# Larger pieces in the halved feed-forward of a two-layer trunk, and modulation vectors spread otherwise over its two stages

## The chip, the cores and the metric

One core of a Trainium2 chip. The metric is the time of one execution in microseconds (us), lower is better; "before" is the median of three runs.

## The reference, cut to what matters

Two layers work on a latent stream x (512 tokens) and a context stream y (256 tokens), both of width 1024. Each layer does a half-step, a mixer and a second half-step. Nine vectors per layer (shift, scale, gate for each of the three) come from `silu(c) @ w_mod[l]` for the latents and `silu(c_ctx) @ w_mod[l]` for the context.

```python
mx = split(silu(c) @ w_mod[l] + b_mod[l], 9)        # my: the same from c_ctx
x = x + 0.5 * mx[2] * swiglu(modulate(rmsnorm(x), mx[0], mx[1]), w1, w3, w2)   # y with my
hx = modulate(rmsnorm(x), mx[3], mx[4])             # hy with my
x = x + mx[5] * mixer(hx, hy);   if not last: y = y + my[5] * ...
x = x + 0.5 * mx[8] * swiglu(modulate(rmsnorm(x), mx[6], mx[7]), ...)
if not last: y = y + 0.5 * my[8] * ...
```

In the last layer the context takes part in the first half-step and in the mixer's keys and values only; `my[5]` to `my[8]` of that layer are not used.

## The kernel before, in words

Activations lie with the features on the partitions. Every fp32 product is made of three fp32r matmuls (`mm3`, L164 to L166) from a high and a low part of each operand; ACT casts the high part of a weight block (L159), DVE subtracts for the low part (L160), up to LOOKAHEAD = 3 blocks ahead. d_ff = 2816 is cut into 22 tiles of 128.

Four feed-forwards run in turn: `ffn` for layer 0's first, `ffn_halved` for layer 0's second and layer 1's first (these two are called stage one and stage two below), `ffn` for layer 1's second. In `ffn_halved` the first WHOLE = 4 tiles are computed plainly; meanwhile DVE and ACT make 24 tiles of differences (T). The other 18 are computed by `up_halved`, which replaces eight block products by seven, each over 384 of the 768 tokens, with DVE and ACT combining results in between (L774, L788, L789, L795 to L803). After every SUB = 2 tiles (the last piece has 4), `down` multiplies g by w2 into PSUM tiles of eight banks, in groups of four (two output tiles, two streams): first with the first tile of the piece for all four, then with the second. Every PSUM result is evicted by ACT with its gate (`add_kept`, L229, tile xpart) and added by POOL's accumulating DMA (L231) to x, which is parked in DRAM (xkept). The last piece adds to x in SBUF on DVE instead.

One pool of 45 slots of 128x512 holds T, g, xpart, the intermediate halves, the vectors' accumulators and x. A halved tile's g takes two slots for the latents and, with its neighbour, two for the context.

The modulation vectors are made beside this on DVE. `mod_chunks` is a generator that loads w_mod in 512 KB chunks through SP's queue into two buffers (wm) and, at a pace in the kernel's own clock of PE work, adds each chunk to two accumulators, one per stream (L319, L321: four instructions per chunk). Four chunks make a half vector, which `mod_fold` transposes and reduces (L329, L330); two halves go through one small matmul (`mod_sums`). The load of chunk i+1 is issued behind the adds of chunk i-1, one buffer being freed by them. Engines work in program order, so an instruction that waits holds up all behind it on its engine.

Stage one carries five vectors of layer 1 at pace 7.4, stage two the other four at pace 9.0. That clock counts 42.8 us for two halved tiles with their down part.

Of the kernel before, what the change touches and what calls it, by code (L numbers as in the profile page):

```python
# [20 lines left out]
DEPTH = 2  # L21
DFF = 2816
NF = DFF // P
PIECES = (4, 4, 4, 4, 2, 4)
# [5 lines left out]
CTX, LAT = 0, 1  # L30
# [10 lines left out]
HK, HN, SUB, WHOLE = KD // 2, NT // 2, 2, 4  # L41
# [3 lines left out]
def per_block(n):  # L45

    return 2 if n * P * 2 <= 1024 else 1
# [34 lines left out]
class Kernel:  # L82
# [229 lines left out]
        yield  # L312
        self.mod_sums(l, j, (half,), rows[:, :32])

    def mod_add(self, acc, raw, k):
        for v in range(2):
            s = self.sc[:, k, v : v + 1]
            if k == 0:
                self.nc.vector.tensor_scalar(acc[v], raw, s, None, op0=ALU.mult)  # L319
            else:  # L320
                self.nc.vector.scalar_tensor_tensor(acc[v], raw, s, acc[v], op0=ALU.mult, op1=ALU.add)  # L321

    def mod_fold(self, acc, rows):

        nc = self.nc
        rv = rows.rearrange("p (v b) -> p v b", v=2)
        for v in range(2):
            t = self.slot("mturn")
            nc.vector.transpose(t, acc[v])  # L329
            nc.vector.tensor_reduce(rv[:, v], t.rearrange("p (b i) -> p b i", i=32), axis=mybir.AxisListType.X, op=ALU.add)  # L330
# [33 lines left out]
    def mod_chunks(self, ljs, pace):  # L364

        nc = self.nc
        steps = [(l, j, half, kk) for l, j in ljs for half in range(2) for kk in range(4)]

        def load():
            raw = self.wide("wm").rearrange("p (k n) -> p k n", k=2)  # L370
            nc.sync.dma_start(raw, self.ins["w_mod"][steps.pop(0)])
            return raw

        after = load()
        for l, j in ljs:
            rows = self.tiny(64, "mrow")
            for half in range(2):
                acc = [self.slot("macc") for _ in range(2)]
                for kk in range(4):
                    raw, after = after, load() if steps else None  # L380
                    yield -pace
                    for k in range(2):
                        self.mod_add(acc, raw[:, k], kk * 2 + k)
                self.mod_fold(acc, rows[:, half * 32 : half * 32 + 32])
            yield 11.71
            self.mod_sums(l, j, (0, 1), rows)

# [138 lines left out]
    def weight_order(self):  # L526

        ins = self.ins

        def halved(l, s):  # L530
            f0 = 0
            for npc in PIECES:
                w2 = ins["w2"][l, s, :, f0 * D : (f0 + npc) * D].rearrange("p (d f n) -> p d f n", d=KD, f=npc)
                sub = npc if f0 + npc == NF else SUB
                for a in range(0, npc, sub):
                    for f in range(f0 + a, f0 + a + sub):
                        both = [ins["w13"][l, s, f, :, m * 1024 : (m + 1) * 1024] for m in range(2)]
                        if f < WHOLE:
                            yield from both
                        else:  # L540
                            yield both
                    per = 8 // sub
                    for d in range(0, KD, per):
                        yield w2[:, d : d + per, a : a + sub]
                f0 += npc

        def ffn(l, s):
            f0 = 0
            for npc in PIECES:
                for f in range(f0, f0 + npc):  # L550
                    for m in range(2):
                        yield ins["w13"][l, s, f, :, m * 1024 : (m + 1) * 1024]
                n = npc * P * per_block(npc)
                for c in range(f0 * D, (f0 + npc) * D, n):
                    yield ins["w2"][l, s, :, c : c + n]
                f0 += npc

        for l in range(DEPTH):
            yield from (halved if (l, 0) in HALVED else ffn)(l, 0)
            for i in range(4, 8) if l < DEPTH - 1 else range(4):  # L560
                yield ins["w_feat"][l, i]
            for i in range(4) if l < DEPTH - 1 else range(4, 8):
                yield ins["w_feat"][l, i]
            for i in range(4):
                yield ins["w_tok"][l, i]
            for i in (10, 11, 12, 13, 8, 9, 14, 15, 16, 17):
                yield ins["w_feat"][l, i]
            for i in range(2):
                for dt2 in range(KD // 2):
                    yield ins["w_out"][l, i, dt2]  # L570
            yield from (halved if (l, 1) in HALVED else ffn)(l, 1)
# [236 lines left out]
    def ffn_halved(self, l, s, h, starts, grps, ends, done):  # L808
        nc = self.nc
        idx = 2 * s  # L810
        accs = {}
        T = {i: [[None] * HK for _ in range(2)] for i in (2, 3, 4)}
        f0 = 0
        while f0 < NF:
            g = self.empty()
            n = SUB if f0 < NF - PIECES[-1] else PIECES[-1]
            last = f0 + n == NF
            per = 8 // n

            def load():  # L820
                for st in (CTX, LAT):
                    self.load_x(st, self.kept[st])

            if f0 < WHOLE:
                if f0 == 0:
                    ws = {f: self.w13() for f in range(n)}
                    for grp in starts[:-1]:
                        self.up(ws, range(n), h, g, grp)
                    self.need(starts[-1])
                    task = self.spawn(self.differences(h, T), 1.0)  # L830
                for f in range(n):
                    if f0:
                        ws = {f: self.w13()}
                    for grp in grps if f0 else starts[-1:]:
                        self.up(ws, [f], h, g, grp)
                if f0 + n == WHOLE:
                    self.drain(task)
                    self.first_difference(h)
            else:
                for f in range(n):  # L840
                    self.up_halved(f, h, T, g, load if last and f == n - 1 else None)
            w2 = []

            def down(dt, grp, ps, fs):
                self.products([(ps, w2[dt // per], dt % per * n * P + fs[0] * P)], g, grp, fs, fs[0] == 0, fs[-1] == n - 1)

            if last:
                w2 = [self.weights() for _ in range(KD // per)]
                for grp in ends:
                    for dt in range(KD):  # L850
                        ps = self.psum("down")[:, : grp[2]]
                        down(dt, grp, ps, range(n))
                        xd = self.xs(dt, grp)
                        nc.vector.scalar_tensor_tensor(xd, ps, self.gate(l, idx, grp[0], dt), xd, op0=ALU.mult, op1=ALU.add)
                        self.square(dt, grp, accs)
                    done(grp, accs)
            else:
                for d in range(0, KD, 2):
                    if d % per == 0:
                        w2.append(self.weights())  # L860
                    these = [(dt, grp, self.psum("down")[:, : grp[2]]) for grp in grps for dt in (d, d + 1)]
                    for fs in ((0,), (1,)):
                        for dt, grp, ps in these:
                            down(dt, grp, ps, fs)
                    for dt, grp, ps in these:
                        self.add_kept(dt, grp, ps, self.gate(l, idx, grp[0], dt))
            f0 += n
# [447 lines left out]
    def run(self):  # L1315
        nc = self.nc
# [62 lines left out]
        later = self.spawn(self.mod_chunks([(0, j) for j in range(3, 9)], 6.0), 80.0)  # L1379
        for l in range(DEPTH):  # L1380
# [9 lines left out]
            if not last:  # L1390
                self.ffn(l, 0, h, both, both, both, done, begun)
                self.drain(later)
                self.decays()
            else:
                later = self.spawn(self.mod_chunks([(l, j) for j in range(5, 9)], 9.0), 90.0)
                self.ffn_halved(l, 0, h, both, both, both, done)
                self.drain(later)

# [1 line left out]
            self.mixer(l, h1, grps, cuts, done)  # L1400

            if not last:
                later = self.spawn(self.mod_chunks([(l + 1, j) for j in range(5)], 7.4), 90.0)
                h, done = next_norm(l + 1, 0)
            else:
                done = self.final
# [136 lines left out]
```

## Time and profile before

| | us |
|---|---|
| runs | 2588.43, 2588.97, 2592.09 (median 2588.97) |
| the profiled execution | 2592.09 |
| its span, first to last instruction | 2590.3 |
| PE busy | 2529.6 (98%) |
| DVE busy | 1811.2 (70%) |
| ACT busy | 1015.7 (39%) |
| POOL busy | 276.6 (11%) |

The profiled execution is the slowest of the three runs; 1.8 us lie outside its span. PE is busy nearly throughout, so what another engine saves counts only where PE waits for it.

### The profile page before, as it was taken

The numbers are of one execution on the slowest core, as the hardware profiler recorded it, in microseconds if no ns is written. First come the engines' busy times: TensorE is split into PE (matmuls) and PEld (weight loads), VectorE is DVE, ScalarE is ACT, GpSimd is POOL, SyncE is SP. The second block draws the span as 40 slices with busy tenths as digits, with TensorE's granted clock in tenths as the row PEclk, the third lists the DMA queues.
The fourth block names the chain that finished last, engine by engine and source line by source line (L and its number), as shares of the span: only waits on it lengthen the run. The fifth ranks groups of instructions, "written<-read, shape, count | busy, mean of one in ns | idle before, by whom it ended". The sixth has DMA issues, their size and how long they took to land. (4 is left out here: it accounts for less than half of the span.)

```text
span 2590.3 us, 36708 instructions
## 1 busy us (share of the span) xinstructions
PE 2529.6 (98%) x14002; PEld 2246.6 (87%) x14002; DVE 1811.2 (70%) x3390; ACT 1015.7 (39%) x1780; POOL 276.6 (11%) x316
## 2 busy tenths in 40 slices
PE   8999999999999999999999999999999999999998
PEld 4888888888888888999899889989998888888887
DVE  6957767747977677788788858758777786633345
ACT  3211211223335444555454445545544263422223
POOL 0000000000000122422320132322310001000000
PEclk9999999999999999999999999999999999999999
DMA  7533433422222745787775457776663334232231
GB/s 273 161 108 122 139 122 114 130 74 100 85 79 60 198 106 130 180 204 180 168 196 187 110 111 195 162 179 179 145 159 122 114 97 119 91 98 98 94 102 41
DMA packets 149265, 345.37 MB, mean 133 GB/s; under 512 B 15712, under 2 KB 54112, under 8 KB 149088
## 3 DMA queue, kind: packets, MB, share of 16 engines
q1 hardware_dynamic: 101088, 276.94, 32.5%
q0 software_dynamic: 44928, 61.89, 15.0%
q10 hardware_dynamic: 3072, 4.20, 0.6%
q8 instruction: 109, 1.79, 0.3%
q14 instruction: 68, 0.56, 0.1%
HBM read 263.27 MB, written 75.50 MB: 131 GB/s over the span
## 5 line engine op out<-in xcount | busy, mean ns | idle before, releaser
L159 ACT CAST wh<-raw 128x1024 fp32r<-128x1024 f32 (+1 forms) x400 | 400.7, 1004 | 863.6 <-PE up L165 329.8
L160 DVE TENSOR_TENSOR wl<-raw,wh 128x1024 fp32r<-128x1024 f32 (+1 forms) x400 | 464.3, 1164 | 338.2 <-ACT wh L159 325.3
L164 PE MATMUL up<-h,wh 128*128 128x512 f32 (+2 forms) x1920 | 663.0, 347 | 21.9 <-ACT half L774 15.7
L165 PE MATMUL up<-h,wh 128*128 128x512 f32 (+2 forms) x1920 | 662.3, 345 | 0.2
L166 PE MATMUL up<-h,wl 128*128 128x512 f32 (+2 forms) x1920 | 661.0, 345 | 0.0
L231 POOL DMA_DIRECT2D xkept<-xpart x312 | 276.4, 1550 | 1904.2 <-ACT xpart L229 1595.0
L164 PE MATMUL down<-g,wh 128*128 128x256 f32 (+1 forms) x1264 | 425.7, 345 | 8.3 <-ACT xpart L229 4.3
L165 PE MATMUL down<-g,wh 128*128 128x256 f32 (+1 forms) x1264 | 431.2, 343 | 0.0
L166 PE MATMUL down<-g,wl 128*128 128x256 f32 (+1 forms) x1264 | 428.2, 341 | 0.4 <-DVE wl L160 0.4
L164 PEld LDWEIGHTS up<-h,wh 128*128 128x128 f32 x1920 | 365.7, 191 | 59.3 <-ACT half L774 17.9
L165 PEld LDWEIGHTS up<-h,wh 128*128 128x128 f32 x1920 | 366.6, 191 | 33.1 <-DVE h L515 0.7
L166 PEld LDWEIGHTS up<-h,wl 128*128 128x128 f32 x1920 | 366.2, 191 | 31.3
L321 DVE SCALAR_TENSOR_TENSOR macc<-wm,sc,macc 128x512 f32<-128x512 f32 x462 | 320.2, 746 | 56.5 <-DMA wm<-in_w_mod_dram 56.3
L164 PEld LDWEIGHTS down<-g,wh 128*128 128x128 f32 x1264 | 236.8, 190 | 41.0 <-ACT g L159 8.3
L165 PEld LDWEIGHTS down<-g,wh 128*128 128x128 f32 x1264 | 240.5, 190 | 28.1 <-DVE g L160 1.7
L166 PEld LDWEIGHTS down<-g,wl 128*128 128x128 f32 x1264 | 239.6, 190 | 28.3 <-DVE wl L160 0.6
L229 ACT ACTIVATE xpart<-down,gate 128x256 f32<-128x256 f32 (+1 forms) x288 | 152.5, 585 | 72.1 <-PE down L166 69.9
L663 DVE TENSOR_TENSOR silu<-silu,up 128x256 f32<-128x256 f32 (+1 forms) x84 | 48.5, 579 | 159.0 <-PE up L166 159.0
L164 PE MATMUL up<-t,wh 128*128 128x384 f32 x432 | 145.2, 336 | 0.3 <-ACT half L774 0.2
L166 PE MATMUL up<-t,wl 128*128 128x384 f32 x432 | 144.4, 334 | 0.0
L165 PE MATMUL up<-t,wh 128*128 128x384 f32 x432 | 144.4, 334 | 0.0
L700 DVE SCALAR_TENSOR_TENSOR x<-down,gate,x 128x512 f32<-128x512 f32 (+1 forms) x152 | 95.0, 634 | 65.9 <-PE down L166 65.2
(210 smaller groups left out, 3298.3 us busy)
## 6 DMA issues: line engine op xcount, KB each, us to landing
raw<-in_w_dram SPq DMA_DIRECT2D x260, 512.0 KB, 3.8
wm<-in_w_mod_dram SPq DMA_DIRECT2D x128, 512.0 KB, 4.3
xkept<-xpart POOLq DMA_DIRECT2D x160, 256.0 KB, 9.3
xkept<-xpart POOLq DMA_DIRECT2D x152, 128.0 KB, 8.6
raw<-in_w_feat_dram SPq DMA_DIRECT2D x36, 512.0 KB, 3.6
xkept<-x SPq DMA_DIRECT2D x44, 256.0 KB, 3.2
x<-xkept SPq DMA_DIRECT2D x44, 256.0 KB, 6.3
wm<-in_w_mod_dram SPq DMA_DIRECT2D x32, 256.0 KB, 5.5
```

The costliest lines, as they stand in the source:

```text
L159: self.nc.scalar.copy(hi, src)
L160: self.nc.vector.tensor_sub(lo, src, hi.bitcast(F32))
L164: nc.tensor.matmul(out, wh, xh, start=start, stop=False, skip_group_check=shared)
L165: nc.tensor.matmul(out, wh, xl, start=False, stop=False, skip_group_check=shared)
L166: nc.tensor.matmul(out, wl, xh, start=False, stop=stop, skip_group_check=shared)
L229: self.nc.scalar.activation(part, ps, AF.Copy, scale=gate)
L231: self.nc.gpsimd.dma_start(self.kept[st][:, c0 : c0 + n], part, accum_op=ALU.add)
L321: self.nc.vector.scalar_tensor_tensor(acc[v], raw, s, acc[v], op0=ALU.mult, op1=ALU.add)
L663: nc.vector.tensor_mul(t, t, ps[f, 1])
L700: nc.vector.scalar_tensor_tensor(xd, ps, self.gate(l, idx, grp[0], dt), xd, op0=ALU.mult, op1=ALU.add)
```

## The change

Pieces of the halved stages become 2, 2, 4, 4, 4, 2, 4 tiles (before: nine of 2, then one of 4). `down` makes its first pass over all tiles of the piece but the last, and its second pass with the last one. The w2 blocks follow: in a piece of four they hold two output tiles by four, in runs of 4 KB in DRAM instead of 1 KB. In the last layer, vectors 5 to 8 are accumulated for the latents alone (two instructions per chunk, one accumulator, a memset in place of the context's fold), at 0.625 of the pace. Stage one carries three vectors at pace 12, stage two six at pace 8 (5.0 for those of the latents alone).

```diff
+    def conditions(l, j):
+        return (LAT,) if l == DEPTH - 1 and j > 4 else (CTX, LAT)
-    def mod_add(self, acc, raw, k):
-        for v in range(2):
+    def mod_add(self, acc, raw, k, vs=(CTX, LAT)):
+        for v in vs:
...
-    def mod_fold(self, acc, rows):
+    def mod_fold(self, acc, rows, vs=(CTX, LAT)):
         for v in range(2):
+            if v not in vs:
+                nc.vector.memset(rv[:, v], 0.0)
+                continue
...
-                acc = [self.slot("macc") for _ in range(2)]
+                vs = self.conditions(l, j)
+                acc = {v: self.slot("macc") for v in vs}
                 for kk in range(4):
                     raw, after = after, load() if steps else None
-                    yield -pace
+                    yield -pace * (0.625 if len(vs) == 1 else 1.0)
                     for k in range(2):
-                        self.mod_add(acc, raw[:, k], kk * 2 + k)
+                        self.mod_add(acc, raw[:, k], kk * 2 + k, vs)
...
-                sub = npc if f0 + npc == NF else SUB
+                sub = SUB if f0 < WHOLE else npc
...
-        while f0 < NF:
+        for n in (SUB,) * (WHOLE // SUB) + PIECES[1:]:
             g = self.empty()
-            n = SUB if f0 < NF - PIECES[-1] else PIECES[-1]
...
-                    for fs in ((0,), (1,)):
+                    for fs in (range(n - 1), range(n - 1, n)):
...
-                later = self.spawn(self.mod_chunks([(l, j) for j in range(5, 9)], 9.0), 90.0)
+                later = self.spawn(self.mod_chunks([(l, j) for j in range(3, 9)], 8.0), 90.0)
...
-                later = self.spawn(self.mod_chunks([(l + 1, j) for j in range(5)], 7.4), 90.0)
+                later = self.spawn(self.mod_chunks([(l + 1, j) for j in range(3)], 12.0), 90.0)
```

## Rows read from the trace of the kernel before

**Rows 1.** The page, part 1: busy time, share of the span, instructions
```profile
PE 2529.6 (98%) x14002; PEld 2246.6 (87%) x14002; DVE 1811.2 (70%) x3390; ACT 1015.7 (39%) x1780; POOL 276.6 (11%) x316
```

**Rows 2.** Windows: length, busy us per engine (instructions), PE clock, DMA share, GB/s
```profile
1002.50:1337.30 334.80, 326.58 (x1857) 309.12 (x1856) 268.76 (x444) 175.67 (x309) 99.07 (x113) 0.99 0.77 185
1542.70:1882.10 339.40, 329.58 (x1856) 311.68 (x1854) 253.14 (x410) 176.40 (x309) 100.42 (x114) 0.98 0.73 175
...
1097.30:1143.60 46.30, 46.30 (x265) 43.85 (x264) 41.86 (x66) 25.27 (x45) 14.78 (x17) 1.00 0.83 197
1189.90:1238.70 48.80, 46.69 (x267) 43.96 (x267) 36.42 (x64) 24.78 (x45) 12.36 (x15) 1.00 0.77 183
1238.70:1290.80 52.10, 47.94 (x265) 45.33 (x265) 40.56 (x63) 25.03 (x45) 14.58 (x17) 0.97 0.70 169
...
1337.30:1394.20 56.90, 56.90 (x325) 55.99 (x324) 51.18 (x81) 27.34 (x48) 4.31 (x5) 1.00 0.69 191
1683.50:1734.60 51.10, 48.16 (x268) 45.60 (x267) 31.83 (x55) 25.16 (x45) 14.17 (x17) 0.97 0.68 162
1882.10:1942.30 60.20, 58.26 (x327) 57.90 (x326) 42.81 (x78) 27.30 (x48) 4.12 (x5) 0.97 0.56 151
...
1080.40:1097.30 16.90, 16.90 (x100) 14.91 (x99) 13.22 (x28) 10.33 (x20) 9.76 (x11) 1.00 0.65 144
```

**Rows 3.** Waits in 1002.5 to 1394.2 (stage one): total us, times, longest
```profile
PE up L164 <- ACT half L774: 4.3, 2, 4.2
PE down L164 <- ACT g L159: 3.9, 2, 2.0
```

**Rows 4.** Waits in 1542.7 to 1942.3 (stage two)
```profile
PE up L164 <- ACT half L774: 11.6, 5, 3.1
DVE macc L321 <- DMA wm<-in_w_mod_dram: 31.2, 8, 6.3
```

**Rows 5.** Timeline around 1699 (DVE, then PE): start, us, what, idle before
```profile
1688.69 2.74 DVE L321 SCALAR_TENSOR_TENSOR macc<-wm,sc,macc 128x512 f32<-128x512 f32 x4 [3.54 <-DMA wm<-in_w_mod_dram]
1694.01 2.74 DVE L321 SCALAR_TENSOR_TENSOR macc<-wm,sc,macc 128x512 f32<-128x512 f32 x4 [2.58 <-DMA wm<-in_w_mod_dram]
...
1697.81 0.55 DVE L788 TENSOR_TENSOR half<-up,half 128x384 f32<-128x384 f32 x1
...
1699.34 0.44 PE L164 MATMUL up<-h,wh 128*128 128x384 f32 x1 [2.94 <-ACT half L774]
```

**Rows 6.** Timeline around 1036 (DVE, then PE)
```profile
1034.90 1.30 DVE L329 STREAM_TRANSPOSE mturn<-macc 128x512 f32<-128x512 f32 x2
1036.12 1.24 DVE L330 TENSOR_REDUCE mrow<-mturn 128x16 f32<-128x512 f32 x2
...
1038.32 0.97 PE L164 MATMUL down<-g,wh 128*128 128x256 f32 x4 [1.95 <-ACT g L159]
```

**Rows 7.** DMA in 1050 to 1337: queues' share of 16 engines; issues, median us to landing
```profile
q0 software_dynamic: 13698, 18.76, 39.9%
q1 hardware_dynamic: 12785, 34.02, 36.1%
...
raw<-in_w_dram SPq DMA_DIRECT2D x37, 512.0 KB, 4.7
wm<-in_w_mod_dram SPq DMA_DIRECT2D x27, 512.0 KB, 6.8
```

**Rows 8.** DMA issues in 150 to 480 (the plain first feed-forward)
```profile
wm<-in_w_mod_dram SPq DMA_DIRECT2D x40, 512.0 KB, 3.5
```

**Rows 9.** The page, part 5: busy us, mean ns, idle before
```profile
L321 DVE SCALAR_TENSOR_TENSOR macc<-wm,sc,macc 128x512 f32<-128x512 f32 x462 | 320.2, 746 | 56.5 <-DMA wm<-in_w_mod_dram 56.3
...
L229 ACT ACTIVATE xpart<-down,gate 128x256 f32<-128x256 f32 (+1 forms) x288 | 152.5, 585 | 72.1 <-PE down L166 69.9
```

**Rows 10.** Tile xpart and the waits, 1002 to 1394: landing, and a wait for it
```profile
DMA to landing us min/median/max: 3.1/10.2/14.2
...
DVE macc L319 <- DMA xkept<-xpart: 2.5, 1, 2.5
```

More of the change, by code (lines that the diff above doesn't have):

```diff
@@ L313, in mod_halfway @@
         self.mod_sums(l, j, (half,), rows[:, :32])
-    def mod_add(self, acc, raw, k):
-        for v in range(2):
+    @staticmethod
+    def conditions(l, j):
+        return (LAT,) if l == DEPTH - 1 and j > 4 else (CTX, LAT)
+    def mod_add(self, acc, raw, k, vs=(CTX, LAT)):
+        for v in vs:
             s = self.sc[:, k, v : v + 1]
@@ L377, in mod_chunks @@
             for half in range(2):
-                acc = [self.slot("macc") for _ in range(2)]
+                vs = self.conditions(l, j)
+                acc = {v: self.slot("macc") for v in vs}
                 for kk in range(4):
                     raw, after = after, load() if steps else None
-                    yield -pace
+                    yield -pace * (0.625 if len(vs) == 1 else 1.0)
                     for k in range(2):
-                        self.mod_add(acc, raw[:, k], kk * 2 + k)
-                self.mod_fold(acc, rows[:, half * 32 : half * 32 + 32])
+                        self.mod_add(acc, raw[:, k], kk * 2 + k, vs)
+                self.mod_fold(acc, rows[:, half * 32 : half * 32 + 32], vs)
             yield 11.71
```

## The prediction

> **What bounds the kernel.** I read the page's busy times first. PE is busy for 98% of the span and the change takes no matmul away, so it can gain only what PE loses by waiting [rows 1]. The second view, windows cut at the borders of the pieces, shows where that is. A piece of two halved tiles with its down part takes 46.3 us when nothing disturbs it; the reader should see that PE is then busy for the whole window [rows 2]; one more window of stage one and three of stage two read 46.3, two read 46.5. Seven such pieces are 7 x 46.3 = 324.1 us. Stage one took 334.8 for them and stage two 339.4, so 10.7 and 15.3 us are lost. The last four halved tiles took 56.9 us in stage one, but 60.2 in stage two: 3.3 more [rows 2]. Together 29.3 us, 1.1% of the time. This is all that the change can win in the part it rebuilds; the first two pieces of each stage keep their order, and so their waits.
>
> The third view, the waits, names two kinds. In stage one PE waited twice in down for a cast of g [rows 3]. Around 1036 the cause can be read off: the fold of a half vector (1.30 + 1.24 us on DVE) stood in front of the last tile's g, and the first pass had ended [rows 6]. The two windows with such a wait took 48.8 us [rows 2] and 48.3: 2.5 + 2.0 = 4.5 us. The other kind is a wait of up for the copy "half": one large one in stage one, five in stage two, 11.6 us of idle [rows 3, 4]. The timeline of one shows the chain: DVE stood still for w_mod twice (3.54 and 2.58 us); then L788 was late, ACT's copies behind it, and PE [rows 5]. Such a window also shows a granted clock of 0.97, that is, PE ran a while at 1.2 instead of 2.4 GHz behind the gap; so a wait of 2 to 3 us costs 4 to 5, as in the window of 51.1 us [rows 2]. This kind cost 52.1 - 46.3 = 5.8 us in stage one and 15.3 + 3.3 = 18.6 us in stage two. The rest, 0.4, is spread.
>
> Why w_mod is late is read from the DMA view. Where no accumulating transfers run, a 512 KB load lands in 3.5 us [rows 8]; beside them the median is 6.8 [rows 7], and an accumulate takes 10.2 [rows 10]. There the accumulates hold 39.9% of all DMA time [rows 7]: of a piece's 46.3 us that is 18.5 us of all 16 engines for its 16 copies, 1.16 each. Down lasts 16.9 us [rows 2]: the copies alone ask for 109% of that, and a queue is left when the next up begins.
>
> The Trainium skill ("DMA: Bandwidth & Descriptors", section "Anatomy of one DMA") fits one transfer with 2.0 us plus its bytes over 436 GB/s, measured for loads issued from GpSimd. By that rule 512 KB would land in an estimated 3.2 us, w_mod would never be late, and the change would win the 4.5 us of the g waits alone, which is the far end of the first rival below (2584). The trace agrees only where no accumulates run [rows 8] and contradicts it beside them [rows 7], so I go by the rows.
>
> **The change part by part.**
>
> *Pieces of four.* Per stage 16 x 3 = 48 evictions, copies and accumulates go, 96 in all: 96 x 0.585 = 56 us of ACT [rows 9] and 96 x 1.16 = 111 us of DMA time. Neither is on PE's path, so by themselves they count nothing. What counts is density. Sixteen accumulates are now spread over two down parts' length, 33.8 us: 18.5 / 33.8 = 55% of DMA time in place of 109%. Weights and w_mod together take 36.1% [rows 7]; split by their numbers of loads (37 and 27) that is 21 and 15. Before, down asked for 109 + 36 = 145%. After, with w_mod scaled by its pace: stage one 55 + 21 + 15 x 7.4/12 = 85%; stage two 55 + 21 + 15 x 7.4/8 = 90% and later, at pace 5, 55 + 21 + 22 = 98%. So the queue behind down should nearly vanish in stage one and be short in stage two. The longer runs of the w2 blocks make it shorter, if anything; bounded by 0 from below, I count nothing.
>
> *First pass over three tiles.* Down has eight passes of 16.9 / 8 = 2.1 us at two tiles. The last g was late by 2.0 to 2.5 us on top of that, 4.6 in all. A first pass over three tiles is 6.3 us, so both waits go: -4.5 us. The piece of tiles 16 and 17 keeps its 2.1.
>
> *Four halved tiles in a row.* DVE no longer gets the rest of a down part after two tiles. The trace has such a stretch: the last four tiles of stage one, at pace 7.4, kept DVE busy for 51.2 of 56.9 us, and PE lost nothing [rows 2]. Pace 8 asks less of DVE, pace 12 much less. Cost 0; if that cover were gone, each us by which DVE falls behind in a tile would be paid by PE.
>
> *Vectors for the latents alone.* Four vectors x 16 k-slices = 64 instructions less, 64 x 0.746 = 48 us of DVE [rows 9], and eight folds of one accumulator, 8 x 1.3 = 10 us [rows 6]; eight small memsets are added. DVE is not the bound: 0 by itself.
>
> *Three and six.* Stage one has 24 chunks in place of 40, stage two 48 in place of 32. From issue to use a chunk has two paces: 24 x 1.08 = 26 us in stage one (1.08 is 46.3 over the 42.8 that the kernel's clock counts), 17 at pace 8, 10.8 at pace 5; before 16 and 19.5. Against a landing of 6.8 in the median stage one is safe: -5.8 us. Stage two isn't: 19.5 us did not prevent five stalls, since DVE runs ahead in down and its adds, and so the next loads, bunch up behind the queue. There the bounds are 0 saved (every stall comes back, 18.6) and 18.6 saved. The stalls stood behind 5 of 7 down parts; four such borders are left. At the same rate and size, 4 x 5/7 x 18.6/5 = 10.6 us would stay; with the queue gone, none. With demand at 90 to 98% in place of 145% I am nearer to none and leave 4 us: -14.6. The chunks of the last vector now end about where the last down begins (the old ones ended some 25 us earlier); the DVE there has the adds to x but PE has eight banks, so 0.
>
> Sum: 4.5 + 5.8 + 14.6 = 24.9, less 1 us that I leave for small new waits on the fuller pool: -24. The profiled execution took 2592.1 (span 2590.3 and 1.8 around it), so 2568; the median of the runs lies 3.1 lower, so 2565.
>
> **The rivals.** *The stalls stay at the borders.* For it: they are behind down parts, and those are twice as long with as many copies queued in a row. Against it: the demand above. Of 14 borders between pieces 8 are left, so 24.4 x 8/14 = 13.9 us remain and 10.5 + 4.5 = 15 are won: 2574; if each stall grows as down does, only the 4.5: 2584.
>
> *Nothing measurable.* At pace 5 a chunk has 10.8 us, and loads beside accumulates already took over 6.8 in half of the cases [rows 7]. If stage two keeps its 18.6 us and each of the four latent vectors adds one stall of 3.7, then 29.3 - 18.6 - 14.8 = -4: about 2589 to 2593. Against it: pace 6 in the first feed-forward, where loads land in 3.5 us [rows 8].
>
> *Slower: the slots run out.* T takes 24 of 45, g of four tiles 12 instead of 6, accumulators 2: in down 7 are left for xpart, before 13. For it: even with 13, DVE once waited 2.5 us for a slot whose copy had not landed [rows 10]. With 7, an eviction reuses the slot of the seventh before it, 9.7 us earlier (bursts of four every 8.4 us); copies take 10.2 in the median. ACT would then wait a little in many bursts. PE pays only when an eviction is later than the 6.3 us for which the other four banks serve, that is, with landings of about 9.7 + 6.3 - 2 (cast and issue) = 14 us, the longest seen [rows 10]. Beyond that each us costs 24 us (3 pieces x 4 bursts x 2 stages); from 1.3 us a burst, 31 us, the gain is used up and the kernel is slower: 2595 to 2610. Against it: at half the density copies should land sooner, not later.
>
> The Trainium skill ("Perfetto Trace Analysis", section "Optimization Strategy") takes the same gap repeating on the engine that should be saturated as a sign that there may not be enough SBUF for the next tile. That would be this rival; the trace of before shows one such wait, on DVE, and none on PE [rows 3, 4, 10].
>
> **How the numbers follow.** 0.2% is 5.2 us, about what a measurement of this kernel can tell from no change: 2584 to 2594. The forecast (18 to 29 us won, 2560 to 2571) has 0.57, stalls that stay (2571 to 2584) 0.23, nothing 0.11, slower 0.09. So faster 0.80, same 0.11, slower 0.09. The range goes from all 29.3 us won, and 1 us of spread between runs, 2558, up into the third case, 2586.
>
> **What would show it.** A piece of four with its down part should take 2 x 46.3 = 92.6 us in the windows; the waits of down for g should be gone; w_mod should land in 4 to 6 us in the median beside the accumulates, and DVE's wait for it in stage two fall from 31.2 us to under 12; PE's clock should read 1.00 in most windows. Right in time but wrong in reason would be: landings as before and stalls gone all the same. The prediction is wrong if PE waits for xpart or ACT for slots in down, or if up still waits for "half" in most pieces of stage two.

## The result and the profile after

The changed kernel takes 2562.37 us in the median of four runs (2560.51 to 2564.37); the kernel before took 2588.70 beside it (four runs, 2587.02 to 2592.09). The ratio is 0.9897, 95% interval 0.9880 to 0.9914: 26.3 us faster, well outside the 0.2% that a measurement can tell. The forecast was 2565, 24 us faster. The profiled execution took 2561.75, its span 2560.0, 30.3 less than the span before.

The page, part 1, and two groups of its part 5 (group, count, busy us and mean ns, idle before them):

```profile
PE 2514.5 (98%) x14002; PEld 2237.3 (87%) x14002; DVE 1761.3 (69%) x3318; ACT 964.0 (38%) x1684; POOL 190.6 (7%) x220
...
L229 ACT ACTIVATE xpart<-down,gate 128x256 f32<-128x256 f32 x192 | 102.6, 585 | 133.9 <-PE down L166 81.8
```

Beside [rows 1] the reader sees the same 14002 matmuls, 96 instructions fewer on ACT and on POOL, and 50 us of DVE less. PE's busy time fell by 15 us with the same count, and its mean granted clock over the span rose from 0.990 to 0.994. None of these figures says what the change was worth; the windows of the rebuilt part do. First come the five pieces of stage one and the five of stage two (length, busy us per engine, PE clock, DMA share, GB/s), then the two stages whole:

```profile
1002.30:1094.20 91.90, 91.90 (x530) 87.78 (x530) 67.64 (x104) 41.89 (x73) 15.12 (x18) 1.00 0.69 162
1094.20:1186.10 91.90, 91.90 (x531) 88.00 (x530) 66.13 (x108) 41.84 (x73) 14.65 (x17) 1.00 0.56 125
1186.10:1279.40 93.30, 92.59 (x532) 88.00 (x531) 65.47 (x108) 41.94 (x73) 14.10 (x17) 1.00 0.59 143
1279.40:1325.40 46.00, 46.00 (x265) 43.91 (x264) 33.61 (x52) 25.14 (x45) 12.72 (x15) 1.00 0.63 156
1325.40:1381.90 56.50, 56.50 (x327) 56.42 (x326) 37.75 (x66) 27.32 (x48) 4.35 (x5) 1.00 0.59 153
1525.30:1617.60 92.30, 92.30 (x531) 87.91 (x530) 75.81 (x124) 41.43 (x73) 17.22 (x20) 1.00 0.71 163
1617.60:1710.60 93.00, 92.60 (x532) 87.96 (x532) 72.62 (x126) 41.97 (x73) 14.13 (x17) 1.00 0.65 169
1710.60:1804.90 94.30, 92.78 (x534) 88.19 (x533) 68.33 (x119) 41.51 (x73) 14.15 (x18) 1.00 0.67 165
1804.90:1854.20 49.30, 46.44 (x265) 43.77 (x264) 33.78 (x51) 24.93 (x45) 12.64 (x15) 1.00 0.72 186
1854.20:1911.20 57.00, 56.90 (x327) 56.30 (x327) 47.72 (x86) 27.45 (x48) 4.34 (x5) 1.00 0.73 193
...
1002.30:1381.90 379.60, 378.89 (x2179) 364.10 (x2179) 270.59 (x438) 178.12 (x308) 60.94 (x70) 1.00 0.61 146
1525.30:1911.20 385.90, 381.01 (x2183) 364.13 (x2182) 298.27 (x506) 177.29 (x308) 62.48 (x71) 1.00 0.69 172
```

Before, the same work took 334.8 + 56.9 = 391.7 us in stage one and 339.4 + 60.2 = 399.6 in stage two [rows 2]. So stage one gave 12.1 us and stage two 13.7: 25.8 of the span's 30.3. The clock reads 1.00 in every one of these windows, where the disturbed ones of before read 0.97 [rows 2]. Of the 4.5 us outside, 2.9 lie in the first two pieces of stage two, whose order the change leaves as it was: 109.7 us at a clock of 0.97 before, 106.8 at 1.00 after, with the same 3.9 us of idle on PE. 1.6 lie elsewhere. These two windows, before and after:

```profile
1433.00:1542.70 109.70, 105.80 (x587) 92.36 (x587) 72.30 (x130) 48.41 (x85) 23.62 (x29) 0.97 0.43 94
...
1418.50:1525.30 106.80, 102.90 (x588) 89.58 (x587) 70.82 (x128) 48.40 (x85) 22.16 (x27) 1.00 0.43 98
```

What is left is read from the same rows: against pieces of 91.9, 46.0 and 56.5, stage one lost 1.4 us and stage two 0.4 + 1.1 + 2.4 + 3.3 + 0.5 = 7.7. The waits name it. Stage one of after (total us, times, longest):

```profile
DVE macc L326 <- DMA wm<-in_w_mod_dram: 5.1, 1, 5.1
...
ACT half L783 <- DMA xkept<-xpart: 1.6, 1, 1.6
...
PE up L164 <- ACT half L783: 0.6, 1, 0.6
```

There is no wait of down for g any more, where [rows 3] had 3.9 us. Stage two of after:

```profile
DVE macc L326 <- DMA wm<-in_w_mod_dram: 21.1, 7, 7.4
...
PE up L164 <- ACT half L783: 4.7, 5, 2.5
```

Against [rows 4], DVE's wait for w_mod fell from 31.2 to 21.1 us and PE's wait behind it from 11.6 to 4.7. The largest one left, from the timeline of after (start, us, what, idle before), is the old chain of [rows 5]:

```profile
1816.18 0.75 DVE L326 SCALAR_TENSOR_TENSOR macc<-wm,sc,macc 128x512 f32<-128x512 f32 x1 [7.37 <-DMA wm<-in_w_mod_dram]
...
1818.77 0.56 DVE L797 TENSOR_TENSOR half<-up,half 128x384 f32<-128x384 f32 x1
...
1819.36 0.52 ACT L798 ACTIVATE half<-half 128x384 f32<-128x384 f32 x1 [4.84 <-DVE half L797]
...
1820.30 0.44 PE L164 MATMUL up<-h,wh 128*128 128x384 f32 x1 [2.53 <-ACT half L783]
```

DVE stood 7.37 us for w_mod; PE, which still had other matmuls to run, stood for 2.53 us behind it. The window around it is 49.3 us long, 3.3 over the quiet one, at a clock of 1.00. The five waits of up lie in three of the five pieces of stage two, the second to the fourth.

The DMA view of 1050 to 1337 in after (share of 16 engines' span; then the issues with the median us to landing) answers to [rows 7]:

```profile
q1 hardware_dynamic: 8044, 29.28, 31.8%
q0 software_dynamic: 9129, 12.45, 31.5%
...
wm<-in_w_mod_dram SPq DMA_DIRECT2D x20, 512.0 KB, 4.4
```

The accumulates' queue went from 39.9% to 31.5% and a w_mod load's landing from 6.8 to 4.4 us. In stage two the same view reads, before and then after:

```profile
wm<-in_w_mod_dram SPq DMA_DIRECT2D x30, 512.0 KB, 7.3
...
wm<-in_w_mod_dram SPq DMA_DIRECT2D x46, 512.0 KB, 4.4
```

### The profile page after: what moved, and what is told of

Same layout as the page of the kernel before. It is cut to its first block, busy times and chain, and to the rows that moved or that the text cites. A ratio compares the mean times of both kernels' runs of the same rounds, so it can differ in the third digit from the quotient of the medians.

```text
span 2560.0 us, 36230 instructions
## 1 busy us (share of the span) xinstructions
PE 2514.5 (98%) x14002; PEld 2237.3 (87%) x14002; DVE 1761.3 (69%) x3318; ACT 964.0 (38%) x1684; POOL 190.6 (7%) x220
## 5 line engine op out<-in xcount | busy, mean ns | idle before, releaser
L166 PEld LDWEIGHTS up<-h,wl 128*128 128x128 f32 x1920 | 362.9, 189 | 31.5
L231 POOL DMA_DIRECT2D xkept<-xpart x216 | 190.4, 1305 | 1959.3 <-ACT xpart L229 1940.5
L326 DVE SCALAR_TENSOR_TENSOR macc<-wm,sc,macc 128x512 f32<-128x512 f32 x406 | 285.4, 747 | 31.4 <-DMA wm<-in_w_mod_dram 30.7
L229 ACT ACTIVATE xpart<-down,gate 128x256 f32<-128x256 f32 x192 | 102.6, 585 | 133.9 <-PE down L166 81.8
```

The lines of the kernel that those rows point to most:

```text
L166: nc.tensor.matmul(out, wl, xh, start=False, stop=stop, skip_group_check=shared)
L229: self.nc.scalar.activation(part, ps, AF.Copy, scale=gate)
L231: self.nc.gpsimd.dma_start(self.kept[st][:, c0 : c0 + n], part, accum_op=ALU.add)
```

## The experiments

The theory: the accumulating copies of down crowd the w_mod loads; the loads come late for DVE, and DVE's lateness reaches PE through the copies "half". Pieces of four thin the copies out and so cure it. Its rivals: the longer lead of the loads from the new spread of the vectors does it (not the pieces); the longer first pass of down does a part; fewer instructions on DVE do it; and, as a limit on the other side, the slots. In the table the lengths are those of the rebuilt part of each stage, from the windows; each median and ratio stands against the kernel before on the same chip (2588.5 us for e1 to e4, 2590.7 for e5 to e8, 2591.0 for e9 to e12).

| run | median us | ratio [95%] | stage one | stage two |
|---|---|---|---|---|
| before | 2588.7 | 1 | 391.7 | 399.6 |
| changed | 2562.4 | 0.9897 [0.9880, 0.9914] | 379.6 | 385.9 |
| e1_pieces | 2558.0 | 0.9880 [0.9866, 0.9893] | 379.1 | 380.4 |
| e2_mods | 2571.3 | 0.9928 [0.9916, 0.9940] | 379.5 | 393.7 |
| e3_pass_one | 2558.4 | 0.9884 [0.9871, 0.9898] | 379.6 | 382.6 |
| e4_no_copies | 2564.5 | 0.9905 [0.9890, 0.9921] | 385.5 | 380.0 |
| e5_before_three | 2569.7 | 0.9923 [0.9909, 0.9936] | 390.4 | 380.5 |
| e6_after_three | 2557.4 | 0.9878 [0.9864, 0.9892] | 378.2 | 384.7 |
| e7_slots41 | 2569.5 | 0.9921 [0.9907, 0.9935] | 382.9 | 387.2 |
| e8_both | 2575.6 | 0.9947 [0.9934, 0.9961] | 378.2 | 400.6 |
| e9_pieces_pass_one | 2559.2 | 0.9879 [0.9864, 0.9894] | 380.1 | 379.2 |
| e10_five_four | 2561.5 | 0.9888 [0.9873, 0.9903] | 379.1 | 382.5 |
| e11_five_four_pass_one | 2562.9 | 0.9891 [0.9874, 0.9907] | 380.0 | 384.9 |
| e12_changed | 2561.7 | 0.9890 [0.9875, 0.9904] | 378.8 | 387.3 |

**e1_pieces: the pieces alone.** The kernel before with pieces of four and the longer first pass; the vectors stay five and four, for both streams.

```diff
-                sub = npc if f0 + npc == NF else SUB
+                sub = SUB if f0 < WHOLE else npc
...
-        while f0 < NF:
+        for n in (SUB,) * (WHOLE // SUB) + PIECES[1:]:
             g = self.empty()
-            n = SUB if f0 < NF - PIECES[-1] else PIECES[-1]
...
-                    for fs in ((0,), (1,)):
+                    for fs in (range(n - 1), range(n - 1, n)):
```

> The kernel before with pieces of four and the longer first pass alone; vectors as before (five at 7.4, four at 9.0, both streams). Queue theory (w_mod is late because accumulates crowd down): both g waits go (4.5 us) and most of the stalls behind down, of 24.4 us some 4 to 8 stay, so 20 to 25 us faster, and w_mod lands in 4 to 5 us in the median. Rival (the vectors' spread is what wins): only the 4.5 us of the g waits, w_mod's waits as before.

Measured 2558.0, 30.5 us faster: all that the whole change wins, and a little more than was expected. Waits of stage two in e1:

```profile
DVE macc L321 <- DMA wm<-in_w_mod_dram: 8.4, 5, 2.9
...
PE up L164 <- ACT half L774: 1.4, 2, 0.7
```

The DMA view of e1, the loads' queue in 1050 to 1337 and the w_mod loads in stage two:

```profile
q1 hardware_dynamic: 9721, 35.37, 37.9%
...
wm<-in_w_mod_dram SPq DMA_DIRECT2D x30, 512.0 KB, 4.2
```

With the vectors, their paces and so the leads of before, DVE's wait is 8.4 us in place of 31.2 and PE's 1.4 in place of 11.6 [rows 4]. The loads land in 4.2 us in stage two (7.3 before). So the pieces alone are enough, and the spread is not needed for the gain. The pieces also bring longer runs in the w2 blocks, and no run separates these from the thinner copies. The rows speak against them: the loads' queue takes 3.0 us of all 16 engines for a MB before (36.1% of 287 us for 34.02 MB [rows 7]) and 3.1 in e1, and e4 below lands its loads early with the old runs.

**e2_mods: the vectors alone.** The changed kernel with the three edits of e1 undone.

```diff
-        for n in (SUB,) * (WHOLE // SUB) + PIECES[1:]:
+        while f0 < NF:
             g = self.empty()
+            n = SUB if f0 < NF - PIECES[-1] else PIECES[-1]
...
-                    for fs in (range(n - 1), range(n - 1, n)):
+                    for fs in ((0,), (1,)):
```

> The changed kernel with the old pieces of two and the old passes; only the vectors are spread and cut. Queue theory: stage one's single stall goes (5.8 us), stage two keeps its five or gets more, since 48 chunks in place of 32 meet the same queue: between 6 us faster and 6 us slower. Rival (spread): 15 to 20 us faster, with stage two's waits for w_mod well under 31 us.

Measured 2571.3, 17.2 us faster: much more than was expected. The stages tell two stories. Windows of e2, stage one and stage two:

```profile
1002.10:1381.60 379.50, 379.45 (x2179) 363.78 (x2178) 269.51 (x436) 203.22 (x356) 103.50 (x118) 1.00 0.72 173
...
1525.10:1918.80 393.70, 383.53 (x2183) 366.51 (x2182) 298.34 (x504) 203.02 (x356) 105.01 (x119) 0.99 0.78 194
```

Its w_mod loads in 1050 to 1337:

```profile
wm<-in_w_mod_dram SPq DMA_DIRECT2D x20, 512.0 KB, 6.8
```

Stage one is cured by the spread alone, down to 0.05 us of idle on PE, though w_mod still lands in 6.8 us there as it did before: at pace 12 a late load is early enough. It gives 12.2 us there where 5.8 were expected, since the two waits for g went as well. Stage two has six vectors and the old copies, and keeps most of its loss: DVE waits 40.3 us for w_mod, PE 9.0 behind it. The two parts give 30.5 and 17.2 us, together 26.3: they cure the same waits, so they don't add.

**e3_pass_one: the changed kernel with a first pass over one tile.**

```diff
-                    for fs in (range(n - 1), range(n - 1, n)):
+                    for fs in (range(1), range(1, n)):
```

> The changed kernel with the first pass of down over one tile and the second over the rest (before the change: one and one). If the longer first pass is what covers a late g: the last g is then needed 2.1 + 0.7 us into down in place of 6.3, and each border where a fold falls on the last tile costs 1 to 2 us: with the two of before, 2 to 5 us slower than the changed kernel. Rival (the folds no longer fall there, the pass matters not): same as the changed kernel within 1 us.

Measured 2558.4, not slower than the changed kernel. No wait of down for g came back in either stage. So the longer first pass is not what took the two waits of [rows 3] away here.

**e4_no_copies: the kernel before without the accumulating copies of the two halved stages.** What it leaves out is that part of the sum into x; the evictions stay.

```diff
-        self.nc.gpsimd.dma_start(self.kept[st][:, c0 : c0 + n], part, accum_op=ALU.add)
+        if self.copies:
+            self.nc.gpsimd.dma_start(self.kept[st][:, c0 : c0 + n], part, accum_op=ALU.add)
```

> The kernel before without the accumulating transfers of the two halved stages (ACT still evicts into xpart, nothing is added to the parked x: that part of the sum is left out). Queue theory: w_mod lands in 3.5 to 4.5 us, all six stalls of up go, the two g waits stay: 22 to 26 us faster than before. Rival (DVE is short of time between the borders whatever the DMA does): stalls stay, under 10 us faster.

Measured 2564.5, 24.0 us faster, as the theory expected. The DMA view of e4 in 1050 to 1337 (loads, size, median us to landing):

```profile
wm<-in_w_mod_dram SPq DMA_DIRECT2D x29, 512.0 KB, 3.6
```

Its waits in stage one (total us, times, longest):

```profile
PE down L164 <- ACT g L159: 3.9, 2, 2.0
...
DVE macc L322 <- DMA wm<-in_w_mod_dram: 2.4, 2, 2.0
```

The load lands in 3.6 us (4.0 in stage two), as it does where no accumulates run [rows 8]; all waits of up for "half" are gone, and stage two takes 380.0 with 0.1 us of idle. The two waits for g stay exactly as they were: they have another cause. This shows the first link of the chain. (Without the copies a slot also comes free sooner; but before, only one wait in stage one, 2.5 us on DVE, stood on a slot [rows 10].) The Trainium skill ("DMA: Bandwidth & Descriptors", section "Issuing engines are not separate DMA queues") says that transfers started by SP, ACT and GpSimd share the same 16 DMA engines and interleave; this run agrees, since GpSimd's copies alone make SP's loads land in 6.8 to 7.3 us in place of 3.6 to 4.0.

**e5_before_three: the kernel before with the loads one chunk further ahead.** A third buffer for w_mod, paid for with two slots.

```diff
-        self.spool = ctx.enter_context(tc.tile_pool(name="slots", bufs=45))
+        self.spool = ctx.enter_context(tc.tile_pool(name="slots", bufs=43))
...
-        after = load()
+        queue = [load(), load()]
...
-                    raw, after = after, load() if steps else None
+                    raw = queue.pop(0)
+                    if steps:
+                        queue.append(load())
...
-        return self.wpool.tile([P, 1024], F32, tag="wm", name=self.name(s), bufs=2)
+        return self.wpool.tile([P, 1024], F32, tag="wm", name=self.name(s), bufs=3)
```

> The kernel before with three w_mod buffers and two loads ahead in place of one; the 4 KB come from two of the 45 slots. Queue theory, in the form that a load has too little lead: a third more lead (three paces, 24 to 29 us) takes most of the six stalls: 12 to 24 us faster, the two g waits stay. Rival (lead does not help, since loads are bunched with the adds and one more transfer joins the queue): within 6 us of before.

Measured 2569.7, 21.0 us faster. The DMA view of e5 in stage two:

```profile
wm<-in_w_mod_dram SPq DMA_DIRECT2D x29, 512.0 KB, 8.0
```

Its waits there:

```profile
DVE macc L321 <- DMA wm<-in_w_mod_dram: 5.9, 4, 3.1
```

The copies are all there and a load lands later than before (8.0 us against 7.3), and yet DVE's wait fell from 31.2 to 5.9 us and stage two from 399.6 to 380.5. So it isn't the landing that costs but the landing beyond the lead, which is half as long again with three paces in place of two (the expectation says a third). In stage one it brought little (390.4): the large wait of up is gone and the two g waits stay (3.9 us), but the two slots are missed. ACT now waits there for slots whose copies had not landed, DVE once for 3.4 us, and PE four times for "half" (2.4 us):

```profile
ACT half L776 <- DMA xkept<-xpart: 10.7, 7, 2.3
```

**e6_after_three: the same three buffers in the changed kernel.** The edit is that of e5.

> The changed kernel with three w_mod buffers and two slots less. What is left of the stalls behind down in stage two (3.5 us at the border after tile 17, some 4 us in smaller ones) should go: 3 to 7 us faster than the changed kernel. Rival (five slots left for xpart are too few): slower than the changed kernel.

Measured 2557.4, the lowest median of all, 4.9 us below the changed kernel with overlapping intervals. DVE's wait for w_mod in stage two is 10.2 us in place of 21.1, but the fold now waits for a slot (11.9 us), and PE's wait for "half" is 3.1 in place of 4.7. The two slots that the buffer cost take back a part.

**e7_slots41: the changed kernel with four slots fewer.**

```diff
-        self.spool = ctx.enter_context(tc.tile_pool(name="slots", bufs=45))
+        self.spool = ctx.enter_context(tc.tile_pool(name="slots", bufs=41))
```

> The changed kernel with 41 slots in place of 45: in down 3 are left for xpart in place of 7. If the changed kernel has room to spare in the pool, ACT and POOL wait for slots, but PE pays less than 1 us a burst: 0 to 15 us slower than the changed kernel. If the pool is near its limit (the slower rival of the prediction), 24 bursts pay 2 us and more: over 45 us slower.

Measured 2569.5, 7.2 us slower than the changed kernel (6 by the ratios, whose intervals touch). Waits of e7 in stage one:

```profile
ACT xpart L229 <- DMA xkept<-xpart: 30.0, 18, 3.3
...
DVE macc L324 <- DMA xkept<-xpart: 7.3, 1, 7.3
...
PE up L164 <- ACT half L783: 3.4, 3, 1.7
```

This is the rival "the slots run out" at work: 18 evictions wait for a slot, 30.0 us in all, and still PE pays only 3.3 us in that stage (382.9 against 379.6). At 45 slots the same view of the changed kernel shows 1.6 us of it, on "half". The rival's mechanism is real, but its point lies below 45 slots. The Trainium skill ("Perfetto Trace Analysis", section "Optimization Strategy") takes a repeating gap on the engine that should be saturated as something that can come from too little SBUF or PSUM for the next tile. Taking slots away does make ACT wait for slots here, but the gaps of before were not of that kind: none stands on a slot [rows 3, 4], and e5 removed those of stage two with two slots fewer.

**e8_both: the changed kernel with vectors 5 to 8 for both streams again, at the same paces.** It has the six vectors of stage two without the saving on DVE.

```diff
     def conditions(l, j):
-        return (LAT,) if l == DEPTH - 1 and j > 4 else (CTX, LAT)
+        return (CTX, LAT)
...
-                    yield -pace * (0.625 if len(vs) == 1 else 1.0)
+                    yield -pace * (0.625 if l == DEPTH - 1 and j > 4 else 1.0)
```

> The changed kernel with the vectors 5 to 8 of the last layer made for both streams again, at the same pace of 5: 64 more accumulates on DVE (48 us) and the folds (10 us) within some 220 us of stage two. If DVE is not the bound there, 0 to 3 us slower than the changed kernel. If the cut to the latents is what makes six vectors fit: a halved tile then asks 9.8 + 7 = 16.8 us of DVE in 14.5 us of PE, and 10 to 25 us are lost in stage two.

Measured 2575.6, 13.3 us slower than the changed kernel, all of it in stage two. Its window there:

```profile
1526.30:1926.90 400.60, 386.12 (x2184) 367.21 (x2184) 344.56 (x578) 176.98 (x308) 61.33 (x70) 0.99 0.65 164
```

DVE has 344.6 us of work in 400.6, and 59.2 in the 67.6 us of the last piece (1859.3 to 1926.9), which took 57.0 in the changed kernel. It waits less for w_mod (14.8 us) and PE more for "half" (7.3). PE also waits 5.4 us, up to 4.4 at a time, for the high part of a weight block: in the longest of these waits, ACT's cast had waited for DVE's differences of the weights (L627), which stood behind four adds of w_mod. Here DVE itself is late. So at these paces three and six can only be had with the latents-alone vectors; both streams at a slower pace were not run.

**e9_pieces_pass_one: e1 with a first pass over one tile.** The edit of e3, on e1.

> Pieces of four with the old spread of the vectors, and the first pass of down over one tile. If the pass over three tiles is what took away the waits for g, folds that fall on a border must now show as waits of down for g: 2 to 5 us slower than pieces of four alone. If the folds merely fall elsewhere once there are half as many borders, the same time within 2 us.

Measured 2559.2, with nearly the interval of e1. Its window of stage one:

```profile
1002.50:1382.60 380.10, 380.10 (x2181) 364.06 (x2180) 321.12 (x526) 179.75 (x308) 60.50 (x70) 1.00 0.65 164
```

PE is busy for all of it: no wait for g here either, with the pace of before. What differs is where the folds fall. In both waits of before the fold starts 2.9 us behind the first matmul of down and stands in front of the last product for g (L803), which so runs 5.3 us behind that matmul. In [rows 6], where this matmul starts at 1032.0:

```profile
1037.28 0.55 DVE L803 TENSOR_TENSOR half<-half,half 128x384 f32<-128x384 f32 x1
```

At four other borders of before a fold starts 0.8 us behind it, and L803 still runs by 3.2; at one, in stage two, the fold starts 4.5 us behind, after L803. None of these five has a wait. In e1 and in e9 no fold starts between 0.8 and 4.9 us behind a border. So the two waits of before are due to where a fold fell, and the pieces and paces move it; no run moved a fold by itself. A late g has other causes as well: the wait of down for g in e2's stage two (1.1 us) and the two of e11 below have no fold in front of them, and DVE had stood for w_mod shortly before each.

**e10_five_four: the changed kernel with the old spread.** Five and four vectors at the old paces; the last four still for the latents alone.

```diff
-                later = self.spawn(self.mod_chunks([(l, j) for j in range(3, 9)], 8.0), 90.0)
+                later = self.spawn(self.mod_chunks([(l, j) for j in range(5, 9)], 9.0 / 0.625), 90.0)
...
-                later = self.spawn(self.mod_chunks([(l + 1, j) for j in range(3)], 12.0), 90.0)
+                later = self.spawn(self.mod_chunks([(l + 1, j) for j in range(5)], 7.4), 90.0)
```

> The changed kernel with the vectors spread five and four again at the old paces (7.4 and 9.0), still for the latents alone in vectors 5 to 8. If moving two vectors into stage two is what makes the changed kernel slower than pieces of four alone: 3 to 6 us faster than the changed kernel, stage two's waits for w_mod under 10 us. Rival (the two differ by chance): equal to the changed kernel within 2 us.

Measured 2561.5, the same as the changed kernel, so the theory that the new spread costs the 4 us between e1 and the changed kernel fell. Beside e1 it differs by the latents-alone vectors, which brought nothing. Waits of e10 in stage two:

```profile
DVE macc L326 <- DMA wm<-in_w_mod_dram: 25.3, 9, 8.4
...
PE up L164 <- ACT half L783: 2.7, 4, 1.3
```

DVE waits 25.3 us for w_mod, more than the 21.1 of the changed kernel, and yet PE waits only 2.7 in place of 4.7. DVE's wait is not the price.

**e11_five_four_pass_one: e10 with a first pass over one tile**, the edit of e3.

> The same with the first pass of down over one tile, so that evictions come one by one, not in bursts of four: if evenly spaced copies land sooner, the last small stalls go and it is 0 to 3 us faster than five and four with the longer first pass; if not, equal. No version so far beats 2557 us by more than the spread of its runs.

Measured 2562.9, as e10 within the intervals. Of the three runs with pieces of four and a first pass over one tile it is the one in which down waited for g, in stage two:

```profile
PE down L164 <- ACT g L159: 1.5, 2, 0.9
```

e10 with the longer pass has no such wait, though its g is as late: at the border after tile 11, the last product for g (L812) runs 3.2 us behind the first matmul of down in either run. So the longer pass does cover a late g, but it was worth no more than 1.5 us.

**e12_changed: the changed kernel again**, on the chip of e9 to e11, without an edit.

> The changed kernel once more, on the chip and beside the runs of these three, so that a few us can be told apart: 2560 to 2565 us if its first median holds.

Measured 2561.7 (2562.4 at first), stages of 378.8 and 387.3: the residue of stage two comes back as it was.

e1, e3, e6 and e9 read 2.5 to 5 us below the changed kernel. That is 0.1 to 0.2%, their intervals overlap with its own, and e10 and e11 contradict the one cause that was tried, so which of them is best, and why, stays open. Any of them beats the kernel before by about 1.2%; the simplest is e1, which leaves the vectors alone.

## Why the prediction was right, and where its steps were not

*What bounds it.* Right: the change won 25.8 us in the rebuilt part, out of what PE had lost there by waiting. The quiet pieces also came out a little shorter than supposed: 91.9 where 2 x 46.3 = 92.6 was said, 46.0 for 46.3, 56.5 for 56.9, 2.8 us a stage. That need not be the pieces' doing: stage one of e2 takes 379.5 with pieces of two and PE busy throughout, where 7 x 46.3 + 56.9 = 381.0 was called undisturbed. What a wait costs was sized by the windows at a clock of 0.97, 4 to 5 us for 2 to 3 of waiting; in after the window with 2.9 us of idle is 3.3 us longer, and its clock reads 1.00. The sum closes with it: 29.3 lost before, plus 2 x 2.8, less the 9.1 left (1.4 and 7.7) is 25.8.

*Density of the copies (step "pieces of four").* The mechanism is right. Removed altogether the copies free the loads (e4), thinned out they do it nearly as well (e1): landing 4.2 to 5.1 us, inside the 4 to 6 that was said. The price was taken as constant, 1.16 us a copy, and is not. Over the whole stages the copies took 37.5% and 37.2% of all DMA time before (118 in each) and 27.1% and 27.0% after (70 and 71), 1.25 us and then 1.47 a copy: some 88 us were freed, not 111.

*The stall of stage one, -5.8.* Gone. It was cured twice over: e1 and e2 each do it alone.

*Stage two, -14.6.* Measured -13.7. The estimate that 4 us stay was low, 7.7 stayed; that and the shorter quiet piece nearly cancel. The bound for DVE's wait (under 12) was wrong: 21.1. It was also the wrong thing to bound, as e10 shows. And of the signs that were to show the prediction wrong, one came: up still waits for "half" in three of the five pieces of stage two. It waits 4.7 us in all in place of 11.6, so the sign, which counts pieces and not time, was badly drawn. The others did not come: in the rebuilt pieces of after PE never waits for xpart, and no wait of ACT for a slot lies in a down part.

*The g waits, -4.5, by the first pass over three tiles.* The amount is right and the reason was not shown. e3 and e9 have the short first pass and no such wait; e2 has it in neither of the two old places, with the old pieces and the old passes. The waits came from folds that happened to start 2.9 us behind a border, and the other edits moved them; that this sum came out is luck as far as the pass goes. Only e11 beside e10 shows the cover at work, for 1.5 us.

*Fewer vectors on DVE, "0 by itself".* Right as worded (e10 beside e1), but it left out what the saving pays for: without it the six vectors of stage two, at the same paces, cost 13.3 us (e8). The step should have said which cover is gone if that edit is.

*What was not in the sum.* 2.9 us in the first two pieces of stage two, where the clock read 0.97 before and 1.00 after. The prediction said that these pieces keep their waits, and they did, 3.9 us; the clock was not in it. Why it fell there before is not shown.

*The rivals.* Stalls that stay at the borders: 9.1 us are left, between the 5 of the forecast (4 and 1) and the 13.9 of this rival, and the largest stands behind a down part, as the rival has it. Nothing measurable: refuted, since stage two didn't keep its 18.6 us. Slots: e7 shows the mechanism, and that it does not decide at 45.

## What to carry to other kernels

Read a late load against its lead, and ask who crowds it: here three edits that share nothing in the code (fewer, larger pieces, a slower pace, a third buffer) each removed the same stall of stage one, so they don't add. Price a stall by what the bounding engine loses in the window around it, not by how long the helper engine waits: 25 us of waiting on DVE cost PE 2.7. When a wait disappears after a change, undo the part to which it was credited; two of this kernel's waits went by an accident of where a fold fell.

## What was unexpected of the hardware

A 512 KB load lands in 3.6 to 4.0 us with no accumulates beside it, in 4.4 with the accumulates at 31.5% of all DMA time, and in 6.8 at 39.9%: a third fewer copies (64 in place of 97), which take a fifth less of DMA time and are spread over longer stretches, take off most of the delay. The Trainium skill ("DMA: Bandwidth & Descriptors", section "Anatomy of one DMA") gives by its fit, made for transfers issued from GpSimd, an estimated 3.2 us. That is near the run without copies; the fit has no term for what else is on the engines.

The accumulates gain as well: from issue to landing the median was 10.2 us before [rows 10] and is 6.7 in stage one of after, with the longest at 12.1 in place of 14.2. That fits with ACT's waits for slots in stage one: a single one of 1.6 us, 5 us into the stage and in no down part, where a reuse after an estimated 9.7 us had been feared. And a third load in flight made each load land later, 8.0 us against 7.3, while the kernel ran 21 us faster.
